# Moving part of the last blocks' cubes from DVE to GpSimd in a row-skewness kernel

## The chip, the cores and the metric

The kernel runs on one core of one Trainium2 chip. The metric is the device time of one execution in microseconds (us), lower is better. Engines are written as the profile writes them: PE (TensorE), DVE (VectorE), ACT (ScalarE), POOL (GpSimd), SP (the engine that issues the transfers here). SBUF and PSUM are the two on-chip memories of the kernel: the transfers fill SBUF, and PE writes its results to PSUM. A transfer's landing is the moment its data are complete in SBUF.

## The reference

```python
def reference(x):                       # x: 1024 x 8192, float32, normal random
    mean = np.mean(x, axis=-1, keepdims=True)
    std = np.std(x, axis=-1, keepdims=True)
    z = (x - mean) / (std + 1e-8)
    return np.mean(z ** 3, axis=-1).astype(np.float32)
```

Each row needs three sums: of x, of its squares and of its cubes. The kernel forms m1 (mean), m2 (mean of squares) and m3 (mean of cubes) and closes with (m3 - 3 m1 (m2 - m1^2) - m1^3) * (m2 - m1^2)^-1.5.

## The kernel before

The 1024 rows are eight blocks of 128 rows, one row per partition. A block's 8192 columns arrive in a few transfers ("units"). For each unit ACT squares the columns and sums the squares, DVE multiplies the squares by x and sums the cubes, and PE adds up the columns of x in 128x128 transposes that accumulate in PSUM. The 128x128 tile that PE accumulates so is copied by ACT (`tsb`) and summed by one more matmul.

```python
UNITS = [
    [4096, 4096], [4096, 4096], [4096, 4096], [4096, 4096],
    [3584, 2304, 2304],
    [2304, 2304, 2048, 1536],
    [1664, 1792, 1920, 1664, 1152],
    [1024, 1024, 1152, 1280, 1408, 1152, 1152],
]
X_BUFS = 8
SQ_BUFS = 4
# ... (cut: pools, constants, close_first_blocks for blocks 0 to 5 on POOL,
#      close_on_act for blocks 6 and 7: six small ACT steps each)
    for b, widths in enumerate(UNITS):
        # ...
        for k, w in enumerate(widths):
            xt = xpool.tile([P, w], FP, tag="x", name=f"x_{b}_{k}")
            nc.sync.dma_start(out=xt, in_=xv[b, :, c0 : c0 + w])
            for s, e in _slices(w):
                # sq is in SBUF; in PSUM for the last unit alone
                nc.scalar.activation(out=sq, in_=xt[:, s:e], func=AF.Square,
                                     scale=s_scale, accum_out=s2u[:, j : j + 1])
                nc.vector.scalar_tensor_tensor(out=cube, in0=sq, scalar=1.0, in1=xt[:, s:e],
                                     op0=ALU.mult, op1=ALU.mult, accum_out=s3u[:, j : j + 1])
            # ... PE: n transposes of 128 columns each, accumulated in tp
        nc.scalar.copy(out=tsb, in_=tp)
        nc.tensor.matmul(out=s1ps[:, b : b + 1], lhsT=tsb, rhs=onesn, start=True, stop=True)
```

Semaphores, and the order of instructions on each engine, are made by the framework's scheduler when the kernel is built. It may move an instruction ahead of others that the source has earlier.

Of the kernel before, what the change touches and what calls it, by code (L numbers as in the profile page):

```python
# [8 lines left out]
FP = mybir.dt.float32  # L9
AF = mybir.ActivationFunctionType  # L10
ALU = mybir.AluOpType
X_AXIS = mybir.AxisListType.X


UNITS = [
    [4096, 4096],
    [4096, 4096],
    [4096, 4096],
    [4096, 4096],
    [3584, 2304, 2304],  # L20
    [2304, 2304, 2048, 1536],
    [1664, 1792, 1920, 1664, 1152],
    [1024, 1024, 1152, 1280, 1408, 1152, 1152],
]
S1_ACT = {(0, 0): 1024, (1, 0): 1024, (2, 0): 1024}
SUB_MAX = 2304
X_BUFS = 8
SQ_BUFS = 4
EARLY = 6


def _slices(w):
    n = -(-w // SUB_MAX)
    step = -(-w // n // 128) * 128
    return [(s, min(s + step, w)) for s in range(0, w, step)]


@with_exitstack
def kernel(
    ctx: ExitStack,  # L40
    tc: tile.TileContext,
    x: bass.AP,
    out: bass.AP,
):
    nc = tc.nc
    P = nc.NUM_PARTITIONS
    R, C = x.shape
    NB = R // P
    L = NB - 1
    F = EARLY  # L50
    inv_n = 1.0 / float(C)
    s_scale = float(C) ** -0.5
    third = (1.0 / 3.0) ** 0.5
    assert len(UNITS) == NB and all(sum(u) == C for u in UNITS)
    nw = len(S1_ACT)
    assert sorted(b for b, _ in S1_ACT) == list(range(nw)) and nw <= F


    xv = x.rearrange("(p b) c -> b p c", b=NB)
    ov = out.rearrange("(p b) -> p b", b=NB)  # L60


    K = max(sum(len(_slices(w)) for w in u) for u in UNITS) + 1

    xpool = ctx.enter_context(tc.tile_pool(name="xp", bufs=X_BUFS))
    sqpool = ctx.enter_context(tc.tile_pool(name="sqp", bufs=SQ_BUFS))
    onep = ctx.enter_context(tc.tile_pool(name="onep", bufs=1))
    psum = ctx.enter_context(tc.tile_pool(name="ps", bufs=2, space=bass.MemoryType.PSUM))
    psum1 = ctx.enter_context(tc.tile_pool(name="ps1", bufs=1, space=bass.MemoryType.PSUM))

    def small(name, n):
        return onep.tile([P, n], FP, tag=name, name=name)

    onesn = small("onesn", 1)
    nc.vector.memset(onesn, inv_n)  # L75
    tiny = small("tiny", 1)
    nc.scalar.activation(out=tiny, in_=onesn, func=AF.Square)  # L77
    ident = small("ident", P)
    make_identity(nc, ident)
    s2u = small("s2u", NB * K)  # L80
    s3u = small("s3u", NB * K)
    nc.vector.memset(s2u, 0.0)
    nc.vector.memset(s3u, 0.0)
    s1a = small("s1a", nw)
    same = small("same", max(S1_ACT.values()))
    junk = small("junk", K)
    expo = small("expo", F)
    nc.gpsimd.memset(expo, -1.5)
    skew = small("skew", NB)
    s1ps = psum1.tile([P, NB], FP, tag="s1ps")  # L90
    m1a = small("m1a", F)
    var2 = small("var2", NB - F)
    Tsb = [small(f"tsb{i}", P) for i in range(2)]

    def close_first_blocks():

        m2, m3 = small("m2a", F), small("m3a", F)
        for dst, src in ((m2, s2u), (m3, s3u)):
            nc.vector.tensor_reduce(  # L99
                out=dst, in_=src[:, 0 : F * K].rearrange("p (b c) -> p b c", c=K),  # L100
                axis=X_AXIS, op=ALU.add,
            )
        m1sq, m1sq3, nm1 = small("m1sqa", F), small("m1sq3a", F), small("nm1a", F)
        nc.scalar.copy(out=m1a[:, nw:F], in_=s1ps[:, nw:F])
        nc.scalar.activation(out=m1sq, in_=m1a, func=AF.Square)
        nc.scalar.activation(out=m1sq3, in_=m1a, func=AF.Square, scale=third)
        nc.scalar.activation(out=nm1, in_=m1a, func=AF.Copy, scale=-3.0)
        g = nc.gpsimd
        var, rr = small("vara", F), small("rra", F)
        g.tensor_tensor(out=var, in0=m2, in1=m1sq, op=ALU.subtract)  # L110
        g.tensor_tensor(out=m1sq3, in0=m1sq3, in1=var, op=ALU.add)  # L111
        g.tensor_tensor(out=m1sq3, in0=m1sq3, in1=nm1, op=ALU.mult)  # L112
        g.tensor_tensor(out=m3, in0=m3, in1=m1sq3, op=ALU.add)  # L113
        g.tensor_tensor(out=rr, in0=var, in1=expo, op=ALU.pow)  # L114
        g.tensor_tensor(out=skew[:, 0:F], in0=m3, in1=rr, op=ALU.mult)  # L115

    def close_on_act(b):

        m2, m1sq, nm1, v3 = (small(f"{t}_{b}", 1) for t in ("m2", "m1sq", "nm1", "v3"))
        p1 = s1ps[:, b : b + 1]  # L120
        var = var2[:, b - F : b - F + 1]
        act = nc.scalar.activation
        yield act(out=junk, in_=s2u[:, b * K : b * K + K], func=AF.Copy, accum_out=m2)
        yield act(out=m1sq, in_=p1, func=AF.Square)  # L124
        yield act(out=var, in_=m1sq, func=AF.Identity, scale=-1.0, bias=m2)  # L125
        yield act(out=nm1, in_=p1, func=AF.Copy, scale=-3.0)  # L126
        yield act(out=v3, in_=m1sq, func=AF.Identity, scale=1.0 / 3.0, bias=var)  # L127
        yield act(  # L128
            out=s3u[:, b * K + K - 1 : b * K + K], in_=v3, func=AF.Identity, scale=nm1
        )  # L130

    pending = iter(())
    for b, widths in enumerate(UNITS):
        tp = psum.tile([P, P], FP, tag="tp", name=f"tp_{b}")
        c0 = 0
        j = b * K
        for k, w in enumerate(widths):
            last_unit = b == L and k == len(widths) - 1
            xt = xpool.tile([P, w], FP, tag="x", name=f"x_{b}_{k}")
            nc.sync.dma_start(out=xt, in_=xv[b, :, c0 : c0 + w])  # L140
            c0 += w
            for s, e in _slices(w):
                if last_unit:
                    sq = psum1.tile([P, e - s], FP, tag="sqps", name=f"sqps_{s}")
                else:
                    sq = sqpool.tile([P, e - s], FP, tag="sq", name=f"sq_{b}_{k}_{s}")
                nc.scalar.activation(  # L147
                    out=sq, in_=xt[:, s:e], func=AF.Square, scale=s_scale,
                    accum_out=s2u[:, j : j + 1],
                )  # L150
                cube = sqpool.tile([P, e - s], FP, tag="sq", name="cube") if last_unit else sq
                nc.vector.scalar_tensor_tensor(  # L152
                    out=cube, in0=sq, scalar=1.0, in1=xt[:, s:e],
                    op0=ALU.mult, op1=ALU.mult, accum_out=s3u[:, j : j + 1],
                )
                j += 1
            w_act = S1_ACT.get((b, k), 0)
            if w_act:
                nc.scalar.activation(  # L159
                    out=same[:, 0:w_act], in_=xt[:, w - w_act : w], func=AF.Copy,  # L160
                    scale=inv_n, accum_out=s1a[:, b : b + 1],
                )
            n = (w - w_act) // P
            for c in range(n):
                nc.tensor.matmul(  # L165
                    out=tp, lhsT=xt[:, c * P : (c + 1) * P], rhs=ident,
                    start=(k == 0 and c == 0), stop=(c0 == C and c == n - 1),
                    is_transpose=True,
                )
            if k > 0:  # L170
                next(pending, None)
                next(pending, None)
        tsb = Tsb[b % 2]
        nc.scalar.copy(out=tsb, in_=tp)  # L174
        nc.tensor.matmul(out=s1ps[:, b : b + 1], lhsT=tsb, rhs=onesn, start=True, stop=True)  # L175
        if b == F - 2:
            nc.vector.tensor_tensor(
                out=m1a[:, 0:nw], in0=s1ps[:, 0:nw], in1=s1a, op=ALU.add
            )
        if b == F - 1:  # L180
            close_first_blocks()
        if b >= F:
            pending = close_on_act(b)
    for _ in pending:
        pass
    rr = small("rr2", NB - F)
    nc.gpsimd.tensor_tensor(out=rr, in0=var2, in1=expo[:, 0 : NB - F], op=ALU.pow)  # L187
    num = small("num2", NB - F)
    nc.vector.tensor_reduce(  # L189
        out=num, in_=s3u[:, F * K :].rearrange("p (b c) -> p b c", c=K), axis=X_AXIS, op=ALU.add  # L190
    )
    nc.vector.tensor_tensor(out=skew[:, F:NB], in0=num, in1=rr, op=ALU.mult)  # L192
    nc.sync.dma_start(out=ov, in_=skew)


# [28 lines left out]
```

## Time and profile before

| | before |
|---|---|
| time, median (4 fast runs) | 91.71 us |
| span of the profiled run | 89.7 us |
| last landing of x | 83.56 us |
| `skew` written | 87.20 us |
| busy: PE, DVE, ACT, POOL | 72%, 81%, 80%, 13% |

A row of busy tenths cuts the span into 40 slices; each digit is how busy the engine was in that slice. A timeline line gives start and length in us, engine, source line, operation and operands. The prediction below shows the lines that carry the reading, so here is only its gist: transfers fill the span, and 3.64 us of closing follow the last landing.

### The profile page before, as it was taken

To read this page: it belongs to the slowest core of one execution; us is meant where nothing else is said; L and a number is where in the kernel's file an instruction comes from. 1 tells how busy PE (TensorE), PEld (TensorE's weight loads), DVE (VectorE), ACT (ScalarE), POOL (GpSimd) and SP (SyncE) were. 2 spreads that over 40 slices of the span, in tenths; PEclk is the share of its full clock that TensorE was granted. 3 is DMA by queue.
4 is the path that set the end of the run, shared out by engine and by line. 5 is a ranking of instruction groups with operands and counts; after the bars stand their busy time and mean duration, and the time that the engine had idled before them with its cause. 6 is when DMAs were issued, how large, how long until landed. Compare 5 with 4: busy or idle time off the path is not lost.

```text
span 89.7 us, 1368 instructions
## 1 busy us (share of the span) xinstructions
PE 64.9 (72%) x504; PEld 59.3 (66%) x504; DVE 72.7 (81%) x80; ACT 72.1 (80%) x106; POOL 11.3 (13%) x14
## 2 busy tenths in 40 slices
PE   0003999892882919989998988888987798969710
PEld 0003999791872909979897977877876787848500
DVE  1000498989999298995999999999999999999970
ACT  6003999699991999859898989978979898999950
POOL 3000000000000000000000000000005999900030
PEclk9999999999999997599999999999999999999998
DMA  3999999999999999999999999999999999994000
GB/s 117 351 424 438 424 431 431 431 431 424 446 416 431 424 438 424 424 438 427 415 409 418 419 427 419 421 415 419 409 414 417 404 413 411 421 412 161 0 0 2
DMA packets 4038, 33.64 MB, mean 375 GB/s; under 512 B 576, under 2 KB 576, under 8 KB 2240
## 3 DMA queue, kind: packets, MB, share of 16 engines
q1 hardware_dynamic: 4032, 33.56, 89.7%
q8 instruction: 4, 0.07, 0.3%
q14 instruction: 2, 0.02, 0.0%
HBM read 33.55 MB, written 0.00 MB: 374 GB/s over the span
## 4 chain that ended last, share of the span: by engine, by line
DMA 73%; ACT 13%; issue 5%; DVE 4%; SPq 1%; PE 1%; DVEq 0%; ACTq 0%
DMA x<-in_x_dram 73%; ACT sq L147 9%; DVE sq L152 3%; ACT sqps L147 1%; ACT same L159 1%; SPq L140 1%; PE s1ps L175 1%; ACT tsb L174 0%; ACT s3u L128 0%; ACT v L127 0%; ACT var L125 0%; DVE num L189 0%; ACT m1sq L124 0%; DVE skew L192 0%; ACT nm L126 0%
## 5 line engine op out<-in xcount | busy, mean ns | idle before, releaser
L152 DVE SCALAR_TENSOR_TENSOR sq<-sq,x 128x2048 f32<-128x2048 f32 (+9 forms) x35 | 70.7, 2071 | 13.4 <-ACT sq L147 13.3
L165 PE MATMUL tp<-ident,x 128*128 128x128 f32 x488 | 62.6, 288 | 17.3 <-DMA x<-in_x_dram 17.2
L165 PEld LDWEIGHTS tp<-ident,x 128*128 128x128 f32 x488 | 57.9, 150 | 20.9 <-DMA x<-in_x_dram 12.7
L147 ACT ACTIVATE sq<-x 128x2048 f32<-128x2048 f32 (+9 forms) x35 | 60.6, 1734 | 10.7 <-DMA x<-in_x_dram 9.9
L110 POOL TENSOR_TENSOR vara<-m2a,m1sqa 128x6 f32<-128x6 f32 x1 | 1.8, 1822 | 67.1 <-DVE m3a L99 67.1
L147 ACT ACTIVATION_READ_ACCUMULATOR sq<-x 128x1 f32 x35 | 6.5, 186 | 0.0
L175 PEld LDWEIGHTS s1ps<-onesn,tsb 128*128 128x128 f32 x16 | 2.4, 188 | 5.2 <-ACT tsb L174 5.2
L175 PE MATMUL s1ps<-onesn,tsb 128*128 128x1 f32 x16 | 3.1, 260 | 3.3 <-ACT tsb L174 3.3
L174 ACT COPY tsb<-tp 128x128 f32<-128x128 f32 x8 | 2.0, 256 | 2.0 <-PE tp L165 2.0
L114 POOL TENSOR_TENSOR rra<-vara,expo 128x6 f32<-128x6 f32 x1 | 3.3, 3267 | 0.0
L159 ACT ACTIVATE same<-x 128x1024 f32<-128x1024 f32 x3 | 3.1, 1041 | 0.0
L152 DVE DVE_READ_ACCUMULATOR sq<-sq,x 128x1 f32 x35 | 2.9, 83 | 0.0
L111 POOL TENSOR_TENSOR m1sq3a<-m1sq3a,vara 128x6 f32<-128x6 f32 x1 | 1.9, 1868 | 0.1
L77 ACT ACT_TABLE_LOAD x1 | 1.3, 1283 | 0.7 <-PEq L208 0.7
L187 POOL TENSOR_TENSOR rr<-var,expo 128x2 f32<-128x2 f32 x1 | 0.7, 702 | 7.7 <-ACT var L125 7.7
L152 DVE SCALAR_TENSOR_TENSOR cube<-sqps,x 128x1152 f32<-128x1152 f32 x1 | 1.4, 1350 | 0.0
L113 POOL TENSOR_TENSOR m3a<-m3a,m1sq3a 128x6 f32<-128x6 f32 x1 | 1.2, 1201 | 0.1
L147 ACT ACTIVATE sqps<-x 128x1152 f32<-128x1152 f32 x1 | 1.1, 1136 | 0.1
L115 POOL TENSOR_TENSOR skew<-m3a,rra 128x6 f32<-128x6 f32 x1 | 1.1, 1069 | 0.1
L124 ACT ACTIVATE m1sq<-s1ps 128x1 f32<-128x1 f32 x2 | 0.3, 171 | 0.5 <-PE s1ps L175 0.5
L75 DVE MEMSET onesn<- 128x1 f32 x1 | 0.1, 59 | 0.8 <-PEq L208 0.8
L112 POOL TENSOR_TENSOR m1sq3a<-m1sq3a,nm1a 128x6 f32<-128x6 f32 x1 | 0.7, 697 | 0.0
(28 smaller groups left out, 6.8 us busy)
## 6 DMA issues: line engine op xcount, KB each, us to landing
x<-in_x_dram SPq DMA_DIRECT2D x8, 2048.0 KB, 23.4
x<-in_x_dram SPq DMA_DIRECT2D x4, 1152.0 KB, 27.9
x<-in_x_dram SPq DMA_DIRECT2D x4, 576.0 KB, 8.6
x<-in_x_dram SPq DMA_DIRECT2D x1, 1792.0 KB, 33.0
x<-in_x_dram SPq DMA_DIRECT2D x2, 832.0 KB, 13.9
x<-in_x_dram SPq DMA_DIRECT2D x1, 1024.0 KB, 21.1
x<-in_x_dram SPq DMA_DIRECT2D x2, 512.0 KB, 10.0
x<-in_x_dram SPq DMA_DIRECT2D x1, 960.0 KB, 13.2
```

The costliest lines, as they stand in the source:

```text
L77: nc.scalar.activation(out=tiny, in_=onesn, func=AF.Square)
L110: g.tensor_tensor(out=var, in0=m2, in1=m1sq, op=ALU.subtract)
L111: g.tensor_tensor(out=m1sq3, in0=m1sq3, in1=var, op=ALU.add)
L113: g.tensor_tensor(out=m3, in0=m3, in1=m1sq3, op=ALU.add)
L114: g.tensor_tensor(out=rr, in0=var, in1=expo, op=ALU.pow)
L115: g.tensor_tensor(out=skew[:, 0:F], in0=m3, in1=rr, op=ALU.mult)
L147: nc.scalar.activation(out=sq, in_=xt[:, s:e], func=AF.Square, scale=s_scale, accum_out=s2u[:, j : j + 1],)
L152: nc.vector.scalar_tensor_tensor(out=cube, in0=sq, scalar=1.0, in1=xt[:, s:e], op0=ALU.mult, op1=ALU.mult, accum_out=s3u[:, j : j + 1],)
L159: nc.scalar.activation(out=same[:, 0:w_act], in_=xt[:, w - w_act : w], func=AF.Copy, scale=inv_n, accum_out=s1a[:, b : b + 1],)
L165: nc.tensor.matmul(out=tp, lhsT=xt[:, c * P : (c + 1) * P], rhs=ident, start=(k == 0 and c == 0), stop=(c0 == C and c == n - 1), is_transp ...
L174: nc.scalar.copy(out=tsb, in_=tp)
L175: nc.tensor.matmul(out=s1ps[:, b : b + 1], lhsT=tsb, rhs=onesn, start=True, stop=True)
```

## The change

Intent: relieve DVE, which is a whole product late at the end. GpSimd makes the cubes of three pieces of 1024 columns, (6,0), (7,0) and (7,3) (block, unit), and PE sums them by transposes, as it sums x. DVE's squares lie in PSUM from (5,3) on, so that its products have one SBUF input. Blocks 0 to 6 are closed together during block 7. There are 31 transfers for 27.

```diff
-    [4096, 4096],
-    [3584, 2304, 2304],
-    [2304, 2304, 2048, 1536],
-    [1664, 1792, 1920, 1664, 1152],
-    [1024, 1024, 1152, 1280, 1408, 1152, 1152],
+    [3584, 2560, 2048],
+    [3072, 2816, 2304],
+    [2816, 1664, 2176, 1536],
+    [1536, 1920, 1920, 1024, 896, 896],
+    [1024, 1024, 1024, 1024, 1024, 1024, 896, 768, 384],
 ]
+POOL = {(6, 0): 1024, (7, 0): 1024, (7, 3): 1024}
+PSUM_FROM = (5, 3)
+PS_MAX, PS_BUFS = 1024, 3
...
+    cube = small("cube", PS_MAX)          # one tile, written by all DVE products from (5,3) on
...
+    def sum_cubes(sq, col):
+        n = sq.shape[1] // P
+        for c in range(n):
+            nc.tensor.matmul(out=gps, lhsT=sq[:, c * P : (c + 1) * P], rhs=ident,
+                start=c == 0, stop=c == n - 1, is_transpose=True)
+        yield
+        nc.scalar.copy(out=gsb, in_=gps)
+        p3 = misc[:, P + NB : P + NB + 1]
+        nc.tensor.matmul(out=p3, lhsT=gsb, rhs=ones, start=True, stop=True)
+        yield
+        nc.scalar.copy(out=s3u[:, col : col + 1], in_=p3)
...
+                if on_pool:
+                    g.tensor_tensor(out=sq, in0=sq, in1=xt[:, s:e], op=ALU.mult)
+                    steps = sum_cubes(sq, j)
+                    later += [(i + 3, steps), (i + 4, steps), (i + 5, steps)]
+                else:
+                    nc.vector.scalar_tensor_tensor(   # out: cube from (5,3) on
...
+            for at, steps in later:
+                if at == i:
+                    next(steps, None)
... (cut: the joint closing after (7,2), the closing of block 7, tp with one buffer for two)
```

`i` counts units: the source asks for the transposes of a piece three units after its product, for the two later steps one unit further on each.

More of the change, by code (lines that the diff above doesn't have):

```diff
@@ L18, with _slices, _plan @@
     [4096, 4096],
-    [4096, 4096],
-    [3584, 2304, 2304],
-    [2304, 2304, 2048, 1536],
-    [1664, 1792, 1920, 1664, 1152],
-    [1024, 1024, 1152, 1280, 1408, 1152, 1152],
+    [3584, 2560, 2048],
[3 more added lines that the diff above has]
+    [1024, 1024, 1024, 1024, 1024, 1024, 896, 768, 384],
 ]
 S1_ACT = {(0, 0): 1024, (1, 0): 1024, (2, 0): 1024}
+POOL = {(6, 0): 1024, (7, 0): 1024, (7, 3): 1024}
+PSUM_FROM = (5, 3)
 SUB_MAX = 2304
+PS_MAX, PS_BUFS = 1024, 3
 X_BUFS = 8
 SQ_BUFS = 4
-EARLY = 6
-def _slices(w):
-    n = -(-w // SUB_MAX)
+EARLY = 7
+EARLY_AT = (7, 2)
+def _slices(w, most):
+    if not w:
+        return []
+    n = -(-w // most)
     step = -(-w // n // 128) * 128
     return [(s, min(s + step, w)) for s in range(0, w, step)]
+def _plan(b, k):
+    w, g = UNITS[b][k], POOL.get((b, k), 0)
+    most = PS_MAX if (b, k) >= PSUM_FROM else SUB_MAX
+    return ([(0, g, True)] if g else []) + [(g + s, g + e, False) for s, e in _slices(w - g, most)]
 @with_exitstack
@@ L53 @@
     third = (1.0 / 3.0) ** 0.5
-    assert len(UNITS) == NB and all(sum(u) == C for u in UNITS)
+    assert len(UNITS) == NB and all(sum(u) == C for u in UNITS) and F == L
     nw = len(S1_ACT)
@@ L60 @@
     ov = out.rearrange("(p b) -> p b", b=NB)
-    K = max(sum(len(_slices(w)) for w in u) for u in UNITS) + 1
+    n_sl = [sum(len(_plan(b, k)) for k in range(len(u))) for b, u in enumerate(UNITS)]
+    K = max(n_sl)
     xpool = ctx.enter_context(tc.tile_pool(name="xp", bufs=X_BUFS))
     sqpool = ctx.enter_context(tc.tile_pool(name="sqp", bufs=SQ_BUFS))
+    gpool = ctx.enter_context(tc.tile_pool(name="gp", bufs=2))
     onep = ctx.enter_context(tc.tile_pool(name="onep", bufs=1))
-    psum = ctx.enter_context(tc.tile_pool(name="ps", bufs=2, space=bass.MemoryType.PSUM))
+    psq = ctx.enter_context(tc.tile_pool(name="psq", bufs=PS_BUFS, space=bass.MemoryType.PSUM))
     psum1 = ctx.enter_context(tc.tile_pool(name="ps1", bufs=1, space=bass.MemoryType.PSUM))
@@ L79 @@
     make_identity(nc, ident)
+    ones = small("ones", 1)
+    nc.gpsimd.memset(ones, 1.0)
     s2u = small("s2u", NB * K)
@@ L89 @@
     skew = small("skew", NB)
-    s1ps = psum1.tile([P, NB], FP, tag="s1ps")
     m1a = small("m1a", F)
-    var2 = small("var2", NB - F)
-    Tsb = [small(f"tsb{i}", P) for i in range(2)]
+    tsb = small("tsb", P)
+    gsb = small("gsb", P)
+    tp = psum1.tile([P, P], FP, tag="tp", name="tp")
+    misc = psum1.tile([P, 2 * P], FP, tag="misc", name="misc")
+    gps = misc[:, 0:P]
+    s1ps = misc[:, P : P + NB]
+    act, g = nc.scalar.activation, nc.gpsimd
     def close_first_blocks():
@@ L103, in close_first_blocks @@
         m1sq, m1sq3, nm1 = small("m1sqa", F), small("m1sq3a", F), small("nm1a", F)
-        nc.scalar.copy(out=m1a[:, nw:F], in_=s1ps[:, nw:F])
-        nc.scalar.activation(out=m1sq, in_=m1a, func=AF.Square)
-        nc.scalar.activation(out=m1sq3, in_=m1a, func=AF.Square, scale=third)
-        nc.scalar.activation(out=nm1, in_=m1a, func=AF.Copy, scale=-3.0)
-        g = nc.gpsimd
+        act(out=m1sq, in_=m1a, func=AF.Square)
+        act(out=m1sq3, in_=m1a, func=AF.Square, scale=third)
+        act(out=nm1, in_=m1a, func=AF.Copy, scale=-3.0)
         var, rr = small("vara", F), small("rra", F)
@@ L115, in close_first_blocks @@
         g.tensor_tensor(out=skew[:, 0:F], in0=m3, in1=rr, op=ALU.mult)
-    def close_on_act(b):
-        m2, m1sq, nm1, v3 = (small(f"{t}_{b}", 1) for t in ("m2", "m1sq", "nm1", "v3"))
-        p1 = s1ps[:, b : b + 1]
-        var = var2[:, b - F : b - F + 1]
-        act = nc.scalar.activation
-        yield act(out=junk, in_=s2u[:, b * K : b * K + K], func=AF.Copy, accum_out=m2)
-        yield act(out=m1sq, in_=p1, func=AF.Square)
-        yield act(out=var, in_=m1sq, func=AF.Identity, scale=-1.0, bias=m2)
-        yield act(out=nm1, in_=p1, func=AF.Copy, scale=-3.0)
-        yield act(out=v3, in_=m1sq, func=AF.Identity, scale=1.0 / 3.0, bias=var)
-        yield act(
-            out=s3u[:, b * K + K - 1 : b * K + K], in_=v3, func=AF.Identity, scale=nm1
-        )
-    pending = iter(())
+    def sum_cubes(sq, col):
+        n = sq.shape[1] // P
+        for c in range(n):
+            nc.tensor.matmul(
+                out=gps, lhsT=sq[:, c * P : (c + 1) * P], rhs=ident,
+                start=c == 0, stop=c == n - 1, is_transpose=True,
+            )
+        yield
[4 more added lines that the diff above has]
+        nc.scalar.copy(out=s3u[:, col : col + 1], in_=p3)
+    later = []
+    i = 0
     for b, widths in enumerate(UNITS):
-        tp = psum.tile([P, P], FP, tag="tp", name=f"tp_{b}")
         c0 = 0
@@ L141 @@
             c0 += w
-            for s, e in _slices(w):
-                if last_unit:
-                    sq = psum1.tile([P, e - s], FP, tag="sqps", name=f"sqps_{s}")
-                else:
-                    sq = sqpool.tile([P, e - s], FP, tag="sq", name=f"sq_{b}_{k}_{s}")
-                nc.scalar.activation(
-                    out=sq, in_=xt[:, s:e], func=AF.Square, scale=s_scale,
-                    accum_out=s2u[:, j : j + 1],
-                )
-                cube = sqpool.tile([P, e - s], FP, tag="sq", name="cube") if last_unit else sq
-                nc.vector.scalar_tensor_tensor(
-                    out=cube, in0=sq, scalar=1.0, in1=xt[:, s:e],
-                    op0=ALU.mult, op1=ALU.mult, accum_out=s3u[:, j : j + 1],
-                )
-                j += 1
-            w_act = S1_ACT.get((b, k), 0)
-            if w_act:
-                nc.scalar.activation(
-                    out=same[:, 0:w_act], in_=xt[:, w - w_act : w], func=AF.Copy,
-                    scale=inv_n, accum_out=s1a[:, b : b + 1],
-                )
+            w_act = S1_ACT.get((b, k), 0)
             n = (w - w_act) // P
@@ L169 @@
                 )
-            if k > 0:
-                next(pending, None)
-                next(pending, None)
-        tsb = Tsb[b % 2]
-        nc.scalar.copy(out=tsb, in_=tp)
-        nc.tensor.matmul(out=s1ps[:, b : b + 1], lhsT=tsb, rhs=onesn, start=True, stop=True)
-        if b == F - 2:
-            nc.vector.tensor_tensor(
-                out=m1a[:, 0:nw], in0=s1ps[:, 0:nw], in1=s1a, op=ALU.add
-            )
-        if b == F - 1:
-            close_first_blocks()
-        if b >= F:
-            pending = close_on_act(b)
@@ L184 @@
-    for _ in pending:
-        pass
-    rr = small("rr2", NB - F)
-    nc.gpsimd.tensor_tensor(out=rr, in0=var2, in1=expo[:, 0 : NB - F], op=ALU.pow)
-    num = small("num2", NB - F)
-    nc.vector.tensor_reduce(
-        out=num, in_=s3u[:, F * K :].rearrange("p (b c) -> p b c", c=K), axis=X_AXIS, op=ALU.add
-    )
-    nc.vector.tensor_tensor(out=skew[:, F:NB], in0=num, in1=rr, op=ALU.mult)
+            if last_unit:
+                nc.scalar.copy(out=tsb, in_=tp)
+            for s, e, on_pool in _plan(b, k):
+                if on_pool:
+                    sq = gpool.tile([P, e - s], FP, tag="gsq", name=f"gsq_{b}_{k}")
+                elif (b, k) >= PSUM_FROM:
+                    sq = psq.tile([P, PS_MAX], FP, tag="psq", name=f"psq_{b}_{k}_{s}")[:, 0 : e - s]
+                else:
+                    sq = sqpool.tile([P, e - s], FP, tag="sq", name=f"sq_{b}_{k}_{s}")
+                act(
+                    out=sq, in_=xt[:, s:e], func=AF.Square, scale=s_scale,
+                    accum_out=s2u[:, j : j + 1],
+                )
+                if on_pool:
+                    g.tensor_tensor(out=sq, in0=sq, in1=xt[:, s:e], op=ALU.mult)
+                    steps = sum_cubes(sq, j)
+                    later += [(i + 3, steps), (i + 4, steps), (i + 5, steps)]
+                else:
+                    nc.vector.scalar_tensor_tensor(
+                        out=cube[:, 0 : e - s] if (b, k) >= PSUM_FROM else sq,
+                        in0=sq, scalar=1.0, in1=xt[:, s:e],
+                        op0=ALU.mult, op1=ALU.mult, accum_out=s3u[:, j : j + 1],
+                    )
+                j += 1
@@ new lines @@
+            if w_act:
+                act(
+                    out=same[:, 0:w_act], in_=xt[:, w - w_act : w], func=AF.Copy,
+                    scale=inv_n, accum_out=s1a[:, b : b + 1],
+                )
+            for at, steps in later:
+                if at == i:
+                    next(steps, None)
+            later = [z for z in later if z[0] > i]
+            if (b, k) == EARLY_AT:
+                nc.vector.tensor_tensor(
+                    out=m1a[:, 0:nw], in0=s1ps[:, 0:nw], in1=s1a, op=ALU.add
+                )
+                nc.scalar.copy(out=m1a[:, nw:F], in_=s1ps[:, nw:F])
+                close_first_blocks()
@@ new lines @@
+            if b == L and k == len(widths) - 2:
+                m2p = small("m2p", 1)
+                act(out=junk[:, 0 : n_sl[L] - 1], in_=s2u[:, L * K : j], func=AF.Copy,
+                    accum_out=m2p)
+            i += 1
+        if b < L:
+            nc.scalar.copy(out=tsb, in_=tp)
+        nc.tensor.matmul(out=s1ps[:, b : b + 1], lhsT=tsb, rhs=onesn, start=True, stop=True)
+    assert not later
+    p1 = s1ps[:, L : L + 1]
+    m1sq, nm1, v3, m2, var, rr, num = (
+        small(f"{t}_l", 1) for t in ("m1sq", "nm1", "v3", "m2", "var", "rr", "num")
+    )
@@ new lines @@
+    g.tensor_tensor(out=m2, in0=m2p, in1=s2u[:, j - 1 : j], op=ALU.add)
+    act(out=m1sq, in_=p1, func=AF.Square)
+    g.tensor_tensor(out=var, in0=m2, in1=m1sq, op=ALU.subtract)
+    g.tensor_tensor(out=rr, in0=var, in1=expo[:, 0:1], op=ALU.pow)
+    act(out=nm1, in_=p1, func=AF.Copy, scale=-3.0)
+    act(out=v3, in_=m1sq, func=AF.Identity, scale=1.0 / 3.0, bias=var)
+    nc.vector.tensor_reduce(out=num, in_=s3u[:, L * K : L * K + n_sl[L]], axis=X_AXIS, op=ALU.add)
+    nc.vector.scalar_tensor_tensor(
+        out=num, in0=v3, scalar=nm1, in1=num, op0=ALU.mult, op1=ALU.add
+    )
@@ L193 @@
+    nc.vector.tensor_tensor(out=skew[:, L:NB], in0=num, in1=rr, op=ALU.mult)
     nc.sync.dma_start(out=ov, in_=skew)
```

## The prediction

> **What bounds the kernel now.** I read the page's rows of busy tenths first. Row DMA is full from the third slice to the last transfer, at some 420 GB/s; no compute engine is ahead of it. The chain that ended last says the same.
>
> ```profile
> DVE  1000498989999298995999999999999999999970
> ACT  6003999699991999859898989978979898999950
> DMA  3999999999999999999999999999999999994000
> ...
> DMA 73%; ACT 13%; issue 5%; DVE 4%; SPq 1%; PE 1%; DVEq 0%; ACTq 0%
> ```
>
> So the 33.55 MB must arrive whatever the engines do, and only what comes after the last landing can be shortened. The timeline's end shows that part.
>
> ```profile
> 83.58 1.14 ACT L147 ACTIVATE sqps<-x 128x1152 f32<-128x1152 f32 x1
> ...
> 83.96 1.35 DVE L152 SCALAR_TENSOR_TENSOR sq<-sq,x 128x1152 f32<-128x1152 f32 x1
> ...
> 84.84 0.27 ACT L174 COPY tsb<-tp 128x128 f32<-128x128 f32 x1
> ...
> 85.16 0.38 PE L175 MATMUL s1ps<-onesn,tsb 128*128 128x1 f32 x2 [0.35 <-ACT tsb L174]
> 85.24 1.35 DVE L152 SCALAR_TENSOR_TENSOR cube<-sqps,x 128x1152 f32<-128x1152 f32 x1
> ...
> 86.44 0.29 ACT L128 ACTIVATE s3u<-v,nm 128x1 f32<-128x1 f32 x1
> ...
> 87.04 0.16 DVE L192 TENSOR_TENSOR skew<-num,rr 128x2 f32<-128x2 f32 x1
> ```
>
> Each line gives start and length in us, engine, line and operation; in brackets stands what the engine idled for. The last unit lands at 83.56 us. DVE is a whole product behind then and ends its cubes at 86.59; ACT's closing chain ends at 86.73; `skew` is done at 87.20, 3.64 us after the landing. The change wants to shorten both strands.
>
> [...]
>
> ```profile
> 68.38 1.82 POOL L110 TENSOR_TENSOR vara<-m2a,m1sqa 128x6 f32<-128x6 f32 x1 [67.07 <-DVE m3a L99]
> ...
> 77.41 1.07 POOL L115 TENSOR_TENSOR skew<-m3a,rra 128x6 f32<-128x6 f32 x1
> ```
>
> The first ends at 70.20, DVE's product of 68.26 + 1.88 at 70.14; the second at 78.48, DVE's of 77.20 + 1.22 at 78.42. Six elements take 1.8 us only because they wait for DVE. [...] Here DVE takes 2289 ns for 2048 columns; no wide GpSimd product is in this trace. [...]
>
> **The change part by part.** DVE loses 3072 columns of 65,536: [...]from the 1024-column row 3 x 1.22 = 3.7 us, enough to remove its lag at the end. Squares in PSUM leave DVE's products one SBUF input, so the lock no longer holds GpSimd. ACT's six small closing steps of block 6 vanish; the new closing after the last landing (square of 384, sum, copy, matmul, square, two GpSimd steps, `skew`), from the rows above, is 0.5 + 0.25 + 0.3 + 0.4 + 0.2 + 0.3 + 0.6 + 0.3, about 3 us even when nothing lags. So the best case gains half a microsecond.
>
> What decides is where the new work stands in the engines' order. The source asks for the sums three units after the product; the built order of the changed kernel does not: on PE the 8 transposes of (6,0)'s cubes stand right behind (6,0)'s own and ahead of (6,1)'s; those of (7,0) are split 6 and 2 around (7,2)'s; those of (7,3) 6 and 2 around (7,5)'s. ACT's copies of the sums stand right behind the squares of (6,1), (7,2) and (7,5). So PE waits for GpSimd with transferred units behind it, and ACT waits for PE. I lay it end to end. Durations: a square costs ACT 0.2 us + 0.833 ns per column (2048 columns: 1.91 start to start), so 1024, 896, 768, 384 columns take 1.05, 0.95, 0.84, 0.52; a transpose costs PE 0.125 (28 in 3.42). Landings: 61,440 columns from 8.18 (first landing) to 83.56, so 1.227 us per 1000; (6,0) ends 14,848 columns before the end: 65.34.
>
> 1. ACT first copies block 5's sums, squares (6,0)'s 1024 from 65.9, done 67.1. GpSimd 2.4: 69.5.
> 2. PE, idle since its transposes of (6,0), does 8 (1.0) and then (6,1)'s 15 (1.9), then the matmul of the sums (0.4): 72.9. ACT's copy waits for that, having finished (6,1) at 69.9. (6,2) landed at 70.05: ACT is now 3 us late.
> 3. ACT squares (6,2) to (6,5), 1.05 + 0.95 + 1.05 + 0.95 + 0.95, and a copy of 0.2: (7,0)'s square starts at 78.1, done 79.25 (landed 74.8; ACT is no faster than the transfers by enough to catch up). GpSimd 2.4: 81.7.
> 4. PE: 6 transposes, (7,2)'s 8, 2 more, 0.25 to drain: 2.25, so 83.95; ACT's copy 0.25: 84.2. ACT stood some 2 us for it.
> 5. (7,3)'s square 1.15: 85.35. GpSimd, which meanwhile did the six closing steps of blocks 0 to 6 (about 2.5 us without the lock: `pow` of six ended 1.3 us after DVE let go at 74.10, the other five I put at 0.2 to 0.25, as the 128x128 memset and select of this trace take 0.2 and 0.3), 2.4: 87.8.
> 6. PE again 2.25: 90.05; copy 0.25: 90.3.
> 7. ACT squares (7,6), (7,7), (7,8): 0.95 + 0.84 + 0.52 + 0.1 = 2.4: 92.7; sum and copy 0.5, matmul 0.4, square 0.2: 93.8; GpSimd's variance 0.25 and `pow` 0.55, hand-overs 0.2, `skew` 0.2: 95.0.
>
> `skew` was done at 87.20, so the path is 7.8 us longer; 91.67 + 7.8 = 99.5 us. The last landing itself hardly moves (83.6 to 84.5).
>
> **The rivals.** A: **it stays with DMA**, GpSimd's products being ready when PE gets to them; then it takes 91.2 to 91.7. For it: DVE loses its lag. Against: the order above, and a product that lands 2.4 us after its square, while PE needs 1.0 us per 1024 columns. B: **GpSimd is much faster**, 1.3 us a product: three products on the path, 3 x 1.1 less, 96.2 us. If a product took no time at all, waiting for PE's other transposes would still leave some 2 us of loss. C: **the lock still holds GpSimd**, or its small steps cost the 0.7 us of the last `pow` (86.16 to 86.86, with DVE free): closing ends after (7,3)'s square, up to 1.8 us more, 101.3. D: **transfers starve**: each buffer of (6,0), (6,1), (6,2) comes free late, so the last transfers are issued 2.5 to 3.5 us ahead of their landing in place of 7.4 and more; DMA may show gaps, but ACT is 4 to 5 us behind the landings by then, so that costs nothing more.
>
> **Range and chances.** A product of 1.6 to 2.9 us moves the sum by -2.4 to +1.5, small GpSimd steps by 0 to +1.8, errors of the laid path by about 1. That gives 99.5, 96.8 to 102.0. Faster needs the order not to bind at all: 0.02. Within 2%: 0.04. Slower: 0.94.
>
> **What the profile will show.** Right: PE waiting for GpSimd's `gsq` three times, 1 to 2.5 us each; ACT's copies of sums waiting for PE, 1 to 2 us each, the first the `s3u` copy in block 6; DVE idle 2 to 3 us three times in the last 25 us (DVE under 80% busy there); GpSimd's 1024-column rows near 2.4 us, its six small closing steps mostly under 0.5; DMA ending near 84 while compute goes on to 95 and the span is near 97.5; the chain that ended last dominated by ACT, PE and POOL at its end. Wrong: GpSimd's rows below 1.3 us; DMA still the last wait before the end; DVE continuously busy to the end.

The path ends with `skew` at 95.0 us, 7.8 later than before, and 91.67 + 7.8 = 99.5 us. The 2.4 us for each GpSimd product of 1024 columns (7.2 us of the path): the trace before has no such product, so this was assumption. The 0.833 ns per column of a square is the slope between two rows of the trace before (1.053 us for 1024 columns, 1.907 for 2048).

"The lock" is the forecast's word for what its two rows of GpSimd show: in the trace before, five of the six small closing steps of blocks 0 to 5 end 0.06 us after a product of DVE with two inputs in SBUF. That a product with its square in PSUM would not hold GpSimd was not shown then; in the changed kernel the step at 81.21 took 0.20 us beside such a product (80.25 to 81.48).

## The result, and the profile after

The changed kernel takes 97.94 us (median of 4 runs, 97.88 to 99.25) against 91.71 us. The ratio is 1.071 (95% interval 1.062 to 1.080); a ratio here is the mean time of one kernel's runs over the mean of the other's of the same rounds, so not quite the ratio of the medians. One run of the four, at 99.25, pulls the mean up. Executions over 1.5% slower than the fastest of the same kernel are left out of the means.

The rows of busy tenths of the changed kernel, with what the transfers moved per slice:

```profile
PE   0005999865988477999497969797299864938710
...
DVE  1000798989892898999999999989883998536480
ACT  6005999699927999999498969899738998490940
...
PEclk9999999999579999999999999999999999999999
DMA  4999999999999999999999999999999989800000
GB/s 109 369 423 437 430 416 430 423 437 437 437 430 430 405 429 423 411 437 423 419 418 426 410 430 413 409 429 412 403 406 409 360 271 339 310 13 0 0 0 2
```

One slice is 2.4 us; PEclk is PE's granted clock in tenths of full speed. DMA is nearly done in slice 35 of 40, at 84 us, and the last piece of x lands at 85.63; the engines then work on alone for 8 us, all of them with holes. None is busy throughout there, so something waits for something. The view of waits names it (engine, line and what it waited for: us in total, times, longest us):

```profile
PE misc L142 <- POOL gsq L185: 5.0, 3, 1.9
DVE cube L189 <- ACT psq L180: 4.7, 3, 2.7
ACT gsb L147 <- PE misc L142: 4.6, 3, 2.4
DVE cube L189 <- ACT s3u L151: 2.1, 1, 2.1
...
ACT s3u L151 <- PE misc L149: 1.5, 1, 1.5
```

L142 is the transposes of GpSimd's cubes, L147 and L151 are ACT's copies of the sums. Read as a chain: PE waits for GpSimd, ACT for PE, DVE for ACT. The timeline shows one turn of it, the last:

```profile
84.42 2.35 POOL L185 TENSOR_TENSOR gsq<-gsq,x 128x1024 f32<-128x1024 f32 x1 [0.81 <-ACT s3u L151]
...
86.82 0.87 PE L142 MATMUL misc<-ident,gsq 128*128 128x128 f32 x6 [1.91 <-POOL gsq L185]
...
87.53 1.04 PE L166 MATMUL tp<-ident,x 128*128 128x128 f32 x8
...
88.41 0.38 PE L142 MATMUL misc<-ident,gsq 128*128 128x128 f32 x2
...
88.88 0.27 ACT L147 COPY gsb<-misc 128x128 f32<-128x128 f32 x1 [2.40 <-PE misc L142]
89.04 0.93 ACT L180 ACTIVATE psq<-x 128x896 f32<-128x896 f32 x1
...
93.58 0.16 DVE L235 TENSOR_TENSOR skew<-num_l,rr_l 128x1 f32<-128x1 f32 x1
```

GpSimd ends at 86.77. PE stood 1.91 us for it although (7,5) had landed at 81.92, some 5 us earlier; it does six transposes, then (7,5)'s eight, then the two that are left; only then may ACT copy. ACT's square of (7,6) starts at 89.04; two more squares and the closing follow it. At this point every byte had been in SBUF for 3.4 us.

### The profile page after: what moved, and what is told of

Same layout as the page of the kernel before. It is cut to its first block, busy times and chain, and to the rows that moved or that the text cites. A ratio compares the mean times of both kernels' runs of the same rounds, so it can differ in the third digit from the quotient of the medians.

```text
span 96.0 us, 1489 instructions
## 1 busy us (share of the span) xinstructions
PE 66.9 (70%) x534; PEld 62.6 (65%) x534; DVE 71.7 (75%) x95; ACT 72.9 (76%) x123; POOL 11.2 (12%) x20
## 5 line engine op out<-in xcount | busy, mean ns | idle before, releaser
L189 DVE SCALAR_TENSOR_TENSOR sq<-sq,x 128x2048 f32<-128x2048 f32 (+7 forms) x26 | 52.3, 2064 | 13.1 <-ACT sq L180 13.0
L180 ACT ACTIVATE sq<-x 128x2048 f32<-128x2048 f32 (+7 forms) x26 | 44.8, 1724 | 10.1 <-DMA x<-in_x_dram 9.2
L189 DVE SCALAR_TENSOR_TENSOR cube<-psq,x 128x1024 f32<-128x1024 f32 (+4 forms) x17 | 18.2, 1068 | 7.9 <-ACT psq L180 4.7
L185 POOL TENSOR_TENSOR gsq<-gsq,x 128x1024 f32<-128x1024 f32 x3 | 7.1, 2358 | 75.7 <-ACT gsq L180 74.9
L180 ACT ACTIVATE psq<-x 128x1024 f32<-128x1024 f32 (+4 forms) x17 | 15.2, 892 | 0.5 <-DMA x<-in_x_dram 0.5
L142 PE MATMUL misc<-ident,gsq 128*128 128x128 f32 x24 | 3.6, 280 | 5.0 <-POOL gsq L185 5.0
L217 PE MATMUL misc<-onesn,tsb 128*128 128x1 f32 x16 | 3.1, 261 | 5.2 <-ACT tsb L216 4.1
L142 PEld LDWEIGHTS misc<-ident,gsq 128*128 128x128 f32 x24 | 2.6, 141 | 5.7 <-POOL gsq L185 5.7
L147 ACT COPY gsb<-misc 128x128 f32<-128x128 f32 x3 | 0.8, 265 | 4.6 <-PE misc L142 4.6
L180 ACT ACTIVATION_READ_ACCUMULATOR psq<-x 128x1 f32 x17 | 3.2, 189 | 0.0
L180 ACT ACTIVATE gsq<-x 128x1024 f32<-128x1024 f32 x3 | 3.2, 1058 | 0.0
L151 ACT COPY s3u<-misc 128x1 f32<-128x1 f32 x3 | 0.5, 153 | 1.5 <-PE misc L149 1.5
```

What stands on the lines that cost most here:

```text
L142: nc.tensor.matmul(out=gps, lhsT=sq[:, c * P : (c + 1) * P], rhs=ident, start=c == 0, stop=c == n - 1, is_transpose=True,)
L147: nc.scalar.copy(out=gsb, in_=gps)
L151: nc.scalar.copy(out=s3u[:, col : col + 1], in_=p3)
L180: act(out=sq, in_=xt[:, s:e], func=AF.Square, scale=s_scale, accum_out=s2u[:, j : j + 1],)
L185: g.tensor_tensor(out=sq, in0=sq, in1=xt[:, s:e], op=ALU.mult)
L189: nc.vector.scalar_tensor_tensor(out=cube[:, 0 : e - s] if (b, k) >= PSUM_FROM else sq, in0=sq, scalar=1.0, in1=xt[:, s:e], op0=ALU.mult, ...
```

## The experiments

Twelve kernels, each run beside the kernel before on the same chip. All gave the reference's result except e2, which is wrong.

### e1: the sums held to the source's places

Edges that fix the order within one engine and wait for nothing else:

```diff
-                nc.tensor.matmul(
+                pe_last = nc.tensor.matmul(
                     out=tp, lhsT=xt[:, c * P : (c + 1) * P], rhs=ident,
...
-                act(
+                act_last = act(
                     out=sq, in_=xt[:, s:e], func=AF.Square, scale=s_scale,
...
                 if at == i:
-                    next(steps, None)
+                    with tc.issue_after(pe_last.ins), tc.issue_after(act_last.ins):
+                        next(steps, None)
```

> The changed kernel with one thing altered: PE's sums of GpSimd's cubes and ACT's copies of them are held to the places where the source asks for them (three, four and five units after the product), by ordering edges that wait for nothing. Same instructions, same GpSimd work. Theory (the place in PE's and ACT's order costs the 6.2 us): PE's waits for gsq fall from 5.0 us in total to under 1, ACT's copies of the sums wait under 1 us in total, the time falls to about 93.3 us (92.0 to 94.5); a rest remains because the sums of (7,3) now fall on the last three units. Rival A (GpSimd's 2.35 us a product is itself too slow, or its work holds DVE): the time stays above 96.5. Rival B (finer transfers and late releases starve DMA): GB/s in the last 15 us stays near 300 and the time above 96.

Measured: 93.49 us (all four runs 93.43 to 93.56), 1.020 times the kernel before. The view of waits:

```profile
ACT gsb L147 <- PE misc L142: 1.0, 1, 1.0
...
PE misc L142 <- POOL gsq L185: 0.5, 1, 0.5
```

The same instructions with the same GpSimd products (2.37 us each) in another order cost 4.4 us less, and PE's wait for GpSimd fell from 5.0 to 0.5 us. That is about seven tenths of the loss, and it is the order alone. Of the 1.85 us that are left, some 1.2 sit at (7,3)'s sum, as expected: so much e2 below, without any sums, is faster, and the one wait for gsq (0.51 us) and ACT's wait for PE (0.96 us) come at 84 to 86 us. The edges move PE's and ACT's steps together; what each engine's order costs alone was not tried.

### e2: products without sums (wrong)

```diff
                     g.tensor_tensor(out=sq, in0=sq, in1=xt[:, s:e], op=ALU.mult)
                     steps = sum_cubes(sq, j)
-                    later += [(i + 3, steps), (i + 4, steps), (i + 5, steps)]
```

> Wrong result on purpose: GpSimd still makes its three products of 1024 columns, but nobody sums them (no transposes of gsq on PE, no copies on ACT). Theory: the products alone cost nothing, 91.5 to 92.5 us, PE and ACT wait for DMA alone. Rival A: if GpSimd's work itself is what costs, the time stays above 95, with DVE's products longer than 1.23 us per 1024 columns while GpSimd works.

Measured: 92.33 us, 1.008 times before. GpSimd still makes three products, and DVE's 1024 columns take 1.23 us throughout. So GpSimd's work does not hold DVE. e2 takes away the work of the sums together with their places; that the places carry most of it is e1's finding. Near the end DVE runs piece behind piece:

```profile
83.05 1.23 DVE L188 SCALAR_TENSOR_TENSOR cube<-psq,x 128x1024 f32<-128x1024 f32 x1
...
84.38 1.09 DVE L188 SCALAR_TENSOR_TENSOR cube<-psq,x 128x896 f32<-128x896 f32 x1
```

The starts are 1.33 us apart, and DVE's last cube ends at 87.18, against 86.59 in the kernel before. That accounts for most of the 0.7 us that remain; e3 and e6 look into it.

### e3: no GpSimd

```diff
-POOL = {(6, 0): 1024, (7, 0): 1024, (7, 3): 1024}
+POOL = {}
```

> The changed kernel with GpSimd taken out: its 3072 columns go to DVE, all else (31 transfers, squares in PSUM from block 5 on, one joint closing) stays. Theory: the waits for gsq vanish; but DVE now has every column in narrow pieces and each product waits for the one before it, since all write the same cube tile (the changed kernel shows 1.32 us from start to start for 1024 columns where the kernel before shows 1.19): DVE falls behind, about 94.5 us (93.0 to 95.5), DVE over 95% busy or waiting on itself to the end. Rival: if the GpSimd part is the only harm in the change, 91.2 to 92.2.

Measured: 95.14 us, 1.038 times before. The rival "only the GpSimd part does harm" falls: without it the change still loses 3.5 us. DVE's timeline near the end:

```profile
83.58 1.23 DVE L189 SCALAR_TENSOR_TENSOR cube<-psq,x 128x1024 f32<-128x1024 f32 x1
...
84.90 1.23 DVE L189 SCALAR_TENSOR_TENSOR cube<-psq,x 128x1024 f32<-128x1024 f32 x1
...
86.22 1.23 DVE L189 SCALAR_TENSOR_TENSOR cube<-psq,x 128x1024 f32<-128x1024 f32 x1
```

The starts are 1.32 us apart. 1024 columns arrive every 1.26 us (1.227 us per 1000 columns), so DVE can't keep up, let alone catch up; it runs without a longer hole to 90.36.

### e6: no GpSimd, two cube tiles

On top of e3:

```diff
-    cube = small("cube", PS_MAX)
+    cubes = [small(f"cube{q}", PS_MAX) for q in range(2)]
...
-                        out=cube[:, 0 : e - s] if (b, k) >= PSUM_FROM else sq,
+                        out=cubes[j % 2][:, 0 : e - s] if (b, k) >= PSUM_FROM else sq,
```

> No GpSimd products, two cube tiles. Theory (without GpSimd the 95.1 us come from DVE waiting on its own last product): start to start 1.19 us, DVE ends 2 to 2.5 us earlier, 92.0 to 92.9 us. Rival (the narrow pieces, three PSUM buffers or the finer transfers are what is slow): stays above 94.

Measured: 92.50 us, 1.011 times before.

```profile
82.80 1.22 DVE L189 SCALAR_TENSOR_TENSOR cube<-psq,x 128x1024 f32<-128x1024 f32 x1
...
83.94 1.22 DVE L189 SCALAR_TENSOR_TENSOR cube<-psq,x 128x1024 f32<-128x1024 f32 x1
```

Starts are now 1.14 us apart. The cube is scratch that nobody reads, but as one tile it makes each product wait until the one before has written it: 1.32 - 1.14, some 0.18 us per product, and 2.6 us in the end. It is a second trap in the change, hidden behind the first. The 1.0 us that is left stands at the same place: DVE runs without a hole from 79.36 and ends its last cube at 87.52, against 86.59 before.

### e5: two cube tiles in the changed kernel

The same edit in the changed kernel, GpSimd and order as they were.

> The changed kernel with two cube tiles written in turn, so that DVE's products no longer wait for the one before. Theory: on the path of the changed kernel DVE isn't the one waited for, so the time stays within 97.4 to 98.3 us, though the start-to-start time of 1024 columns falls from 1.32 to about 1.19 where DVE has work. Rival: DVE's narrow self-waiting products carry the loss: then 95 or less.

Measured: 97.62 and 97.64 us in the two fast runs, ratio 1.066; two slow runs at 99.4 are left out. In its trace the starts of 1024 columns are 1.15 us apart. On the path of the changed kernel DVE is not waited for, so taking its self-wait away gives 0.3 us. The order of repairs matters: this edit is worth 2.6 us without GpSimd and next to nothing with it.

### e9, e10, e11: one product at a time

Two cube tiles throughout, the scheduler's own order; against e6 (92.50):

```diff
-POOL = {(6, 0): 1024, (7, 0): 1024, (7, 3): 1024}
+POOL = {(6, 0): 1024}      # e9;  e10: {(7, 0): 1024};  e11: {(7, 3): 1024}
```

> Two cube tiles, GpSimd's product at (6,0) alone, its sum where the scheduler puts it (ahead of (6,1)'s transposes). Without GpSimd this was 92.50 us. If each product's misplaced sum costs by itself, this one costs 1.0 to 2.2 us: 93.5 to 94.7. If the three only cost together (a rival: the late state must build up), 92.9 or less.

> The same with GpSimd's product at (7,0) alone: its sum is split around (7,2)'s transposes. Expected 0.5 to 1.7 us above the 92.50 without GpSimd: 93.0 to 94.2.

> The same with GpSimd's product at (7,3) alone, whose sum stands ahead of (7,5)'s transposes with nothing after it to catch up in: 1.8 to 3.0 us above 92.50: 94.3 to 95.5. The three increments together should come to 4.3 to 6 us, which with the 1.0 us of the version without GpSimd makes the 6.1 us of the change with two cube tiles.

Measured: e9 93.82 (+1.3), e10 93.39 (+0.9), e11 96.28 (+3.8). Each misplaced sum costs by itself; nothing has to build up. e11 missed its range by 0.8 us, and the three increments make 6.0 where 4.3 to 6 were expected and the change with two cube tiles has 97.6 - 92.5 = 5.1. The trace of e11 shows what fell on it. PE around its wait:

```profile
83.92 1.54 PE L142 MATMUL misc<-ident,gsq 128*128 128x128 f32 x6 [2.67 <-POOL gsq L185]
85.25 1.91 PE L166 MATMUL tp<-ident,x 128*128 128x128 f32 x8
```

Six transposes take 1.54 us where the changed kernel took 0.87, eight 1.91 where it took 1.04. The view of stretches gives PE's granted clock (stretch in us; its length, busy time and instructions of PE, PEld, DVE, ACT, POOL; then the clock, DMA share and GB/s):

```profile
84.00:85.50 1.50, 1.50 (x8) 1.50 (x9) 0.88 (x2) 0.00 (x0) 0.00 (x0) 0.50 0.00 0
85.20:87.20 2.00, 2.00 (x12) 2.00 (x11) 0.00 (x0) 0.00 (x0) 0.00 (x0) 0.52 0.00 0
87.20:89.40 2.20, 2.15 (x20) 1.92 (x18) 0.69 (x1) 1.93 (x6) 0.00 (x0) 1.00 0.00 0
```

After standing 2.67 us PE works at half clock (0.50 and 0.52) to about 87.1 us, and then at 1.00. The length of the wait alone does not decide: in e4 below PE stood 2.63 us before 84.63 and then took 0.85 us for six transposes (the changed kernel 0.87 at full clock), while the changed kernel has 0.50 from 24 to 27 us (the 5 and 7 in its row PEclk) after a wait of 2.08 us for a transfer.

The traces of the kernel before and of the changed kernel show more. Each has one stretch of half clock ahead of its last matmul, of 3.41 us: 34.62 to 38.03 us before, 23.95 to 27.36 in the changed kernel. In the 3.41 us ahead of it PE was busy for 1.35 us (before) and 1.34 us (changed). If the two traces are cut into stretches of that length from there, back to 14 us and on to the start of the last matmul, no other stretch has less than 1.60 us of busy PE (before, 20.97 to 24.38) or 1.51 us (changed, 30.78 to 34.19), and full clock followed each. In e11 PE was busy for about 0.9 us of the 3.41 us before its half clock set in at about 83.7 (0.97 on the mean of 80 to 84 us, 0.50 from 84). In the changed kernel ACT and PE arrived later, so PE waited 1.74, 1.31 and 1.91 us, was busy for at least 1.98 us of every stretch from 61.5 to 92.2 us, and kept full clock.

From the lengths I estimate that half clock cost e11 (1.54 - 0.87) + (1.91 - 1.04), about 1.5 us. Without it e11 would have been near 94.8, inside what was expected, and the three increments near 4.5.

### e4: DVE's squares in SBUF

```diff
-PSUM_FROM = (5, 3)
+PSUM_FROM = (8, 0)
```

> The changed kernel with DVE's squares in SBUF to the end, so that DVE's products have two SBUF inputs while GpSimd works. If the lock [...]holds for these, GpSimd's 1024-column products last clearly longer than 2.36 us where DVE is busy beside them (3 us or more for at least one), or DVE's are stretched, and the six small closing steps take 1 us and more instead of 0.2; the time is then 98.5 to 101. If there is no such lock between products of this kind, 97.5 to 98.3 as in the changed kernel, with 2.36 us a product.

Measured: 101.45 us in one run, 103.2 to 103.6 in three, the profiled one among them; so no ratio is given, and only durations are read. They are enough for the lock. POOL and DVE around (6,0), from their two timelines:

```profile
66.74 3.53 POOL L185 TENSOR_TENSOR gsq<-gsq,x 128x1024 f32<-128x1024 f32 x1 [65.39 <-ACT gsq L180]
```

```profile
66.30 1.75 DVE L189 SCALAR_TENSOR_TENSOR sq<-sq,x 128x1536 f32<-128x1536 f32 x1
...
67.98 2.83 DVE L189 SCALAR_TENSOR_TENSOR sq<-sq,x 128x512 f32<-128x512 f32 x1
```

GpSimd stands until DVE's product ends at 68.05 and then has its own 2.2 us, to 70.27; DVE's 512 columns, 0.69 us in the changed kernel, stand until GpSimd ends and are done at 70.81. Here each stood until the other had ended. So the PSUM part of the change does what it is for, and the place alone cost DVE next to nothing: a product of 1024 columns took 1225 ns with its square in PSUM (the changed kernel) and 1223 ns with both inputs in SBUF (the kernel before). Two expectations were missed. The time was to be at most 101; PE stood 2.98 and 2.73 us for gsq in this trace, and half clock followed the first (0.50 from 70.3 to 72.3 us) and, by the lengths, the second (six transposes in 1.54 us). And the six closing steps were to take 1 us and more: only two were stretched (0.52 and 1.16 us), the others took what they take in the changed kernel. The edit also makes DVE's pieces wider (up to 1920 columns where the changed kernel has at most 1024), so it is not the place of the squares alone; the rows above compare pieces of equal width.

### e8: more x buffers

```diff
-X_BUFS = 8
-SQ_BUFS = 4
+X_BUFS = 10
+SQ_BUFS = 3
```

> The changed kernel with ten x buffers (and three square buffers) in place of eight and four, same order on PE and ACT: transfers no longer wait for late releases. Theory: DMA keeps 400 GB/s and more to its end and the last landing comes back to about 83.6, but the time stays at 97.5 to 98.4, since ACT is 4 us and more behind the landings. Rival (starved transfers cost the time): 95.5 or less.

Measured: 97.72 us, ratio 1.067. The row of GB/s of e8:

```profile
GB/s 109 376 417 438 438 431 424 431 438 438 424 417 424 426 416 416 426 446 417 422 411 424 407 429 426 405 424 417 400 410 411 409 411 395 92 0 0 0 0 2
```

The dip to 271 GB/s of the changed kernel is gone, the last landing is at 83.80 in place of 85.63, and the time doesn't follow. The dip is a result of late releases, and costs at most the 0.2 us between 97.94 and 97.72.

### e12: the 31 transfers in the kernel before

`UNITS` of the change in the kernel before, nothing else.

> The kernel before with one part of the change alone: its 27 transfers replaced by the 31 of the change. If the transfers' sizes are harmless, 91.4 to 92.1 us (four more transfers, a last one of 384 columns for 1152); the last landing near 83.7 us. Rival: if finer transfers cost DMA time, 92.5 and more.

Measured: 91.58 us, ratio 1.001 (0.999 to 1.002). The finer transfers are neutral.

### e7: what the experiments point to

e1's order, two cube tiles, and no product at (7,3):

```diff
-POOL = {(6, 0): 1024, (7, 0): 1024, (7, 3): 1024}
+POOL = {(6, 0): 1024, (7, 0): 1024}
```

> The version that the experiments point to: sums in the source's order, two cube tiles, GpSimd's products at (6,0) and (7,0) alone, none at (7,3) where its sums fall on the last units. Theory: last landing near 83.6, skew near 87.6: 91.6 to 92.4 us, that is, no more than a return to the kernel before, because the last landing stays and the closing after it is no shorter. A gain would be 91.0 or less.

Measured: 91.94 us, ratio 1.0045 (1.003 to 1.006) over five rounds: mended, the change comes back to the kernel before, and stays 0.4 us behind it. In its trace DVE and ACT end their last pieces one behind the other:

```profile
84.72 0.48 ACT L180 ACTIVATE psq<-x 128x384 f32<-128x384 f32 x1
...
86.34 0.55 DVE L189 SCALAR_TENSOR_TENSOR cube<-psq,x 128x384 f32<-128x384 f32 x1
...
87.54 0.16 DVE L236 TENSOR_TENSOR skew<-num_l,rr_l 128x1 f32<-128x1 f32 x1
```

`skew` is written at 87.70, against 87.20 before. The last unit lands at 83.92, ACT takes it up 0.8 us later, and DVE, which has run without a hole since 78.7 us, takes it up 1.1 us after the end of ACT's square. No version that I ran beats the kernel before. With the last landing at 83.56 before and 83.92 here, only the closing behind it (3.64 us before) is left to shorten; whether another version could gain there was not tried.

## Why the prediction was right

**Time and direction.** 97.94 lies inside 96.8 to 102.0, 1.6 us below the 99.5 of the sum. Slower was given 0.94. Each step of the path below was right to 0.4 us, so the hit is not luck.

**The order as the cause.** The step that carried the prediction was the reading of the built order: sums of gsq ahead of units that the source has earlier, on engines that stood at it with landed units behind (PE 1.91 us, ACT 2.40 us at the last sum). e1 shows it by altering the order alone (4.4 of 6.2 us), e2 by leaving the sums out, work and place together (5.6 us), e9 to e11 piece by piece.

**The path, step by step.** In us from the span's start:

| end of step | predicted | measured |
|---|---|---|
| 1: GpSimd's first product | 69.5 | 69.3 |
| 2: ACT's square of (6,2) starts | 72.9 | 72.3 |
| 3: second product | 81.7 | 81.0 |
| 4: ACT's square of (7,3) starts | 84.2 | 83.2 |
| 5: third product | 87.8 | 86.8 |
| 6: ACT's square of (7,6) starts | 90.3 | 89.0 |
| 7: `skew` written | 95.0 | 93.7 |

The 1.3 us of difference come mostly from steps 2, 4 and 6 (0.4, 0.3 and 0.2): the matmul of the sums took 0.28 and not 0.4, fifteen transposes 1.80 and not 1.9 (and the terms of step 2 add to 72.8, not 72.9), the sixteen transposes of steps 4 and 6 with their drain 1.96 and not 2.25, and ACT's copies overlapped the next square (0.16 us from start to start in place of 0.25). Steps 1 and 3 give 0.2 each, steps 5 and 7 nothing. The other 0.3 us of the 1.6 lie outside the path: from `skew` to the end the span has 2.5 us before and 2.3 after. The mechanism held; the small hand-over terms were each rounded up.

**GpSimd's durations.** The 2.4 us assumed for 1024 columns was near: 2.35 to 2.37. The small closing steps took 0.19 to 0.21 us, the `pow` of one column 0.56 and of seven 1.51 (of two 0.70 in the kernel before), so rival C fell. Rival B would have needed 1.3 us a product and fell with it. Rival D came much as described: gaps in the transfers (271 to 360 GB/s), the last five transfers issued 4.1 to 4.6 us ahead of their landing where 2.5 to 3.5 was expected, and e8 shows that they cost next to nothing.

**Where it was wrong.** The best case was mis-sized: "the best case gains half a microsecond", and rival A at 91.2 to 91.7. With the order mended and three products the kernel takes 93.49, with two and two cube tiles 91.94. The prediction took the closing from the last landing with nothing lagging; it did not see DVE's self-wait on the cube tile (0.18 us per product). "The last landing itself hardly moves (83.6 to 84.5)" was wrong: it came at 85.63; the path did not run through it, so this cost the prediction nothing. Of the signs, PE's three waits and GpSimd's rows came as said, but ACT's wait for the last sum was 2.40 us and not 1 to 2 (and 0.42 for the first), one of DVE's three holes 1.74 and not 2 to 3, and the span 96.0 and not 97.5. And the chain that ended last was to show ACT, PE and POOL at its end; the page's chain of the changed kernel reaches back only over the last 1.5 us, all DVE, and shows none of the three. The waits and the timeline had to do.

**Left open.** The run at 99.25 us and the two at 99.4 us of e5 are 1.3 to 1.8 us above their fellows, close to the 1.5 us that half clock cost e11. That PE sometimes falls to half clock in these runs is only argued; they have no traces of their own.

## What to carry to other kernels

Where work goes from one engine to another and its result comes back, read the built order on the engine that takes it back: in the changed kernel PE waited there three times, 5.0 us in all, the last time with a unit behind that had landed some 5 us before PE went on, and the gap in the source between product and use says nothing if a scheduler may close it. Fix such an order with edges within the engine, and put no late partner's result on the last units. Give scratch outputs that nobody reads at least two buffers (one cost 0.18 us per product here), and keep PE's waits short: in e11 half clock followed one of 2.67 us and cost about 1.5 us more.
